# An MLP's first product by seven block products in place of eight, in a tuned fp32 transformer step

## Chip, cores and metric

One core of a Trainium2 chip runs the kernel. The metric is the device time of one launch in microseconds (us): the median of several runs. A measurement of this kernel tells about 0.2% from no change.

## What is computed

The reference is one step of a two-layer model on 640 tokens (128 of context, 512 latent) of width 1024. Each layer modulates its input, projects it, runs three kinds of attention heads, projects the result, and ends in a squared-ReLU MLP with 4096 features. The change lies in the MLP; `w_mlp1` is 1024 x 4096, `w_mlp2` is 4096 x 1024:

```
def _residual_tail(x, mix_heads, g_a, sh_m, sc_m, g_m, w_out, ln1_g, ln1_b, w_mlp1, w_mlp2, ln2_g, ln2_b):
    mix = jnp.concatenate(mix_heads, axis=-1) @ w_out
    x = _layer_norm(DN_ALPHA * x + g_a * mix, ln1_g, ln1_b)
    h = x * (1.0 + sc_m) + sh_m
    f = jnp.square(jax.nn.relu(h @ w_mlp1)) @ w_mlp2
    return _layer_norm(DN_ALPHA * x + g_m * f, ln2_g, ln2_b)
```

## The kernel before

Everything is fp32, and every large product is made from split operands: a number is the sum of a rounded part (hi, fp32r) and the rest (lo), and each product of two 128-deep blocks is three matmuls, hi·hi, lo·hi and hi·lo. `piece` (L366 to L373) makes a split weight: a DMA of 256 KB on SyncE's queue (SP) into one of four raw buffers (`wrawt`), ScalarE's cast to hi (L371), VectorE's subtraction to lo (L372), into one of eight buffers (`wst`). The split itself is

```
        nc.scalar.copy(ws[:, 0, :], raw)
        nc.vector.tensor_tensor(out=ws[:, 1, :], in0=raw, in1=ws[:, 0, :].bitcast(F32), op=ALU.subtract)
```

The MLP's input, transposed to features by tokens, is `Xt`: eight depth blocks of 128, hi and lo, 640 tokens. `to_feat` fills it one token tile of 128 at a time: four transposes on TensorE, four activations on ScalarE with the modulation's scale and bias, a cast (L509) and a subtraction (L510).

`mlp` (L1243 to L1313) goes through the 32 feature blocks in four chunks of eight. In a chunk `gemm_feat` (matmuls on L459) forms the first product: for a block two halves of 320 tokens, 24 matmuls of 320 columns each into a PSUM bank `gfeat`, 48 for a block. ScalarE copies each half out (L1257), VectorE squares the ReLU over 640 columns (L1258), ScalarE casts to hi (L1261) and GpSimd subtracts to lo (L1262): the split `f1T`, the stationary operand of the second product. That is `gemm_tok` (matmuls on L387), twice for a chunk, once for each half of 512 output columns: five token tiles, eight feature blocks, three matmuls of 512 columns each, 240 for a chunk. VectorE adds each finished tile to the residual from PSUM (`ln_add`, L1169 to L1176). In the first chunk VectorE also finishes the layer norm before (`ln_half`, L1237 and L1238, 20 operations of 128x512).

TensorE's order is written out by a planner when the program is built; the other engines' order comes from a scheduler, and each engine runs its own queue in order. After the last matmul of the second layer only the last tile's layer norm and its store remain.

Of the kernel before, what the change touches and what calls it, by code (L numbers as in the profile page):

```python
# [18 lines left out]
L = 2  # L19
D = 1024  # L20
NT = 5
TOK = 640
# [78 lines left out]
class Net:  # L101
# [277 lines left out]

    def gemm_tok(self, A, src, n, evac, by_block=False):  # L380

        nc = self.nc
        ws = [self.piece(src[:, k, :], n) for k in range(8)]

        def mm(o, t, k):
            for hl, wl in ((0, 0), (1, 0), (0, 1)):
                nc.tensor.matmul(  # L387
                    o, lhsT=A[YORDER[k] if A is self.Y else k][:, hl, t * 128 : (t + 1) * 128], rhs=ws[k][:, wl, :],
                    start=(k == 0 and hl + wl == 0), stop=(k == 7 and wl == 1),
                )  # L390

        if by_block:
# [101 lines left out]

    def to_feat(self, xh, t, A, B):

        nc = self.nc
        s = 1 if t == 0 else 0
        sl = slice(t * 128, (t + 1) * 128)
        for q in range(2):  # L500
            pt = self.tp.tile([128, 4, 128], F32, tag="t", name="pth")
            v = self.sm.tile([128, 4, 128], F32, tag="val", name="val", bufs=2)
            for j in range(4):
                k = 4 * q + j
                nc.tensor.transpose(pt[:, j, :], xh[:, k * 128 : (k + 1) * 128], self.ident)
# [223 lines left out]
    def mlstm(self, l):  # L729
# [119 lines left out]
        def chain():  # L849
# [27 lines left out]
            ce = self.sm.tile([128, 512], F32, name="ctxCe", bufs=1)  # L877
            nc.scalar.copy(ce[0:65, :], cp[0:65, :])
# [285 lines left out]
    def ln_add(self, r, q, o, gr, alpha, st=None, v=None):  # L1164
# [3 lines left out]
        v = o if v is None else v  # L1168
        nc.vector.tensor_tensor(out=v, in0=o, in1=gr[:, qs], op=ALU.mult)  # L1169
        o = v  # L1170
# [16 lines left out]
    def tail1(self, l, xsrc):  # L1187
# [9 lines left out]
        for t in range(NT):  # L1197
            self.R.append(self.qk.tile([128, D], F32, tag="qk", name="res"))
            nc.sync.dma_start(self.R[t], xsrc(t))
            st.append(self.sm.tile([128, 2, 6], F32, tag="bst", name="bst", bufs=NT))  # L1200

        def ev(q):
            def f(t, o):
                r = self.R[t]
                v = None if q else self.sm.tile([128, 512], F32, tag="val", name="wov", bufs=2)
                self.ln_add(r, q, o, g[:, int(t == 0)], ALPHA, st[t] if q else None, v)
                if q == 0 and t == NT - 1:
# [20 lines left out]
    def ln_half(self, l, i, h, dst=None):  # L1228
# [12 lines left out]
        self.use("V", 6.8)  # L1241

    def mlp(self, l):  # L1243
        nc, I, O = self.nc, self.I, self.O
        NC = 4
        last = l == L - 1
        R = self.R
        st = {}
        for c in range(NC):
            ft = []  # L1250
            n0 = 4 if c == 0 else 2
            first = [I["w1"][l, c * 8 + j] for j in range(n0)]
            rest = (g for j in range(n0, 8) for g in self.gemm_feat(I["w1"][l, c * 8 + j]))
            for j, g in enumerate(itertools.chain(self.gemm_feat(*first), rest)):
                f = self.tmp.tile([128, 2, 320], F32, tag="tmp", name="f1")
                for h in range(2):
                    nc.scalar.copy(f[:, h], g[h])  # L1257
                nc.vector.scalar_tensor_tensor(out=f, in0=f, scalar=0.0, in1=f, op0=ALU.max, op1=ALU.mult)  # L1258
                ft.append(self.yp.tile([128, 2, TOK], F32R, tag="y", name="f1T"))
                y = ft[j].rearrange("p a (h t) -> p a h t", h=2)  # L1260
                nc.scalar.copy(y[:, 0], f)  # L1261
                nc.gpsimd.tensor_tensor(out=y[:, 1], in0=f, in1=y[:, 0].bitcast(F32), op=ALU.subtract)  # L1262
                self.use("A", 0.75, self.use("V", 0.85, self.use("A", 0.9, self.T + 0.3)))
                if c == 0 and j in (3, 5):
                    self.ln_half(l, 0, j // 2 - 1)
            if c == 0:
                self.drain()
                if not last:
                    for i in range(3):
                        self.add(self.ada(l + 1, i, 512, 9.5), "ada")  # L1270
                gl = self.rowbc(self.pp, "p", self.ada_r[l][0:1, 5 * D : 6 * D])
                gc = self.rowbc(self.pp, "p", self.ada_r[l][1:2, 5 * D : 6 * D])
                if last:
                    lg = self.rowbc(self.pp, "p", I["ln"][l, 2:3, :])
                    lb = self.rowbc(self.pp, "p", I["ln"][l, 3:4, :])
            if c == NC - 1:
# [35 lines left out]
            for q in range(2):  # L1312
                self.gemm_tok(ft, I["w2"][l, c, q], 512, ev(q))  # L1313

# [68 lines left out]
def _pack(inp):  # L1383
# [89 lines left out]
```

## Time and profile before

| | |
|---|---|
| median of three runs | 1755.53 us (1752.77 to 1756.3) |
| profiled execution, its own time | 1749.54 us |
| its span, first to last instruction | 1747.8 us |
| mean granted TensorE clock | 0.98 of full speed |
| busy: TensorE, VectorE, ScalarE, GpSimd | 95%, 55%, 38%, 11% |
| MLP of the first layer begins, of the second | 418 us, 1281 us |

In the profile PE is TensorE, PEld its weight loads (beside PE), DVE VectorE, ACT ScalarE, POOL GpSimd, SP SyncE, which issues the loads. L459 is line 459 of the kernel. An idle time is given with what ended it: "0.51 <-ACT f L1257" is 0.51 us of waiting for ScalarE's write of `f` on line 1257. Matmul durations overlap in the pipeline, so the pace is read from the starts of successive groups.

### The profile page before, as it was taken

Reading aid. Unit: us, or ns where it says so; the run is one execution under the profiler, and the core shown is the slowest. Engines: PE = TensorE matmul, PEld = TensorE weight load, DVE = VectorE, ACT = ScalarE, POOL = GpSimd, SP = SyncE. Lnnn points to the kernel's source line nnn. Section 1 sums busy time; section 2 is a strip of 40 time slices with the busy share of each in tenths; the row PEclk is TensorE's granted clock in tenths of the full one; section 3 lists DMA queues with packets and bytes.
Section 4 is the critical chain, followed back from the end, with each engine's and each line's share of the span. In section 5 each row is a group of like instructions: output and inputs, shape, how many; then the busy total and the mean of one; then the engine's idle time right before and its main releaser. Section 6 shows DMA issues by size and latency. Waiting matters only on the chain.

```text
span 1747.8 us, 27703 instructions
## 1 busy us (share of the span) xinstructions
PE 1655.0 (95%) x10708; PEld 1439.3 (82%) x10708; DVE 954.8 (55%) x2105; ACT 660.0 (38%) x1482; POOL 189.8 (11%) x152
## 2 busy tenths in 40 slices
PE   5999799999999999999999997999999999999996
PEld 4988587778978878879889886878789898898985
DVE  3467766669533334233385777675784433433438
ACT  2342466655412313213253424665463142231420
POOL 0051000000300201101100510000002011020110
PEclk9999899999999999999999998999999999999998
DMA  8544433332344445433224331221322231221312
GB/s 312 200 154 142 138 130 114 108 115 90 110 140 168 163 145 170 151 103 109 67 88 143 98 98 41 74 73 60 127 80 90 65 98 62 91 73 49 103 44 83
DMA packets 105279, 195.23 MB, mean 112 GB/s; under 512 B 16410, under 2 KB 43034, under 8 KB 100028
## 3 DMA queue, kind: packets, MB, share of 16 engines
q1 hardware_dynamic: 105148, 193.47, 34.2%
q8 instruction: 84, 1.38, 0.3%
q14 instruction: 47, 0.39, 0.1%
HBM read 185.16 MB, written 8.26 MB: 111 GB/s over the span
## 4 chain that ended last, share of the span: by engine, by line
PE 74%; DVE 11%; issue 5%; DMA 4%; ACT 4%; POOL 1%; SPq 0%; DVEq 0%; ACTq 0%; POOLq 0%
PE gtok L387 34%; PE gfeat L459 30%; PE adaps L244 2%; PE o L1029 2%; PE ptp L1013 2%; ACT P L984 2%; PE s L970 1%; DMA adab<-in_b_ada 1%; DVE nm L977 1%; DVE wst L372 1%; DVE P L991 1%; DMA wrawt<-in_w_f 1%; DMA adaw<-in_w_ada 1%; PE mli L790 1%; POOL f1T L1262 1%
## 5 line engine op out<-in xcount | busy, mean ns | idle before, releaser
L459 PE MATMUL gfeat<-Xt,wst 128*128 128x320 f32 x4416 | 682.0, 313 | 6.6 <-ACT Xt L509 3.1
L459 PEld LDWEIGHTS gfeat<-Xt,wst 128*128 128x128 f32 x4416 | 655.2, 190 | 27.4 <-issue 11.6
L387 PE MATMUL gtok<-wst,f1T 128*128 128x512 f32 x1920 | 452.6, 396 | 0.9 <-ACT wst L371 0.8
L387 PEld LDWEIGHTS gtok<-wst,f1T 128*128 128x128 f32 x1920 | 359.1, 188 | 96.0 <-issue 8.4
L371 ACT CAST wst<-wrawt 128x512 fp32r<-128x512 f32 (+2 forms) x392 | 233.1, 604 | 513.9 <-PE gtok L387 253.2
L372 DVE TENSOR_TENSOR wst<-wrawt,wst 128x512 fp32r<-128x512 f32 (+2 forms) x392 | 272.7, 707 | 281.2 <-ACT wst L371 279.9
L1262 POOL TENSOR_TENSOR f1T<-f,f1T 128x640 fp32r<-128x640 f32 x64 | 105.1, 1642 | 976.5 <-ACT f1T L1261 973.8
L1169 DVE TENSOR_TENSOR gtok<-gtok,row 128x512 f32<-128x512 f32 x90 | 62.8, 698 | 226.5 <-PE gtok L387 226.1
L387 PE MATMUL gtok<-wst,Xt 128*128 128x384 f32 (+1 forms) x720 | 125.9, 330 | 7.4 <-DVE wst L372 7.4
L387 PEld LDWEIGHTS gtok<-wst,Xt 128*128 128x128 f32 x720 | 116.3, 193 | 11.3 <-DVE wst L372 8.6
L387 PE MATMUL gtok<-wst,yT 128*128 128x512 f32 x480 | 117.8, 399 | 1.6 <-DVE wov L1169 1.6
L1257 ACT COPY f<-gfeat 128x320 f32<-128x320 f32 x128 | 54.3, 426 | 154.0 <-PE gfeat L459 145.8
L387 PEld LDWEIGHTS gtok<-wst,yT 128*128 128x128 f32 x480 | 88.3, 188 | 22.9 <-DVE wov L1169 2.4
L984 ACT ACTIVATE P<-P,nm 128x512 f32<-128x512 f32 (+2 forms) x120 | 80.6, 673 | 33.5 <-DVE nm L979 15.7
L1258 DVE SCALAR_TENSOR_TENSOR f<-f 128x640 f32<-128x640 f32 x64 | 52.7, 823 | 53.3 <-ACT f L1257 53.3
L977 DVE TENSOR_REDUCE nm<-P 128x2 f32<-128x1024 f32 (+2 forms) x60 | 66.5, 1109 | 15.6 <-ACT P L1066 8.6
L244 PE MATMUL adaps<-adaw,cs 128*32 128x512 f32 (+1 forms) x576 | 56.1, 497 | 19.2 <-DMA adaw<-in_w_ada 19.1
L1021 ACT COPY PT<-ptp 128x512 f32<-128x512 f32 (+1 forms) x120 | 61.1, 542 | 24.9 <-PE ptp L1013 24.5
L1013 PE MATMUL ptp<-ident,P 128*128 128x128 f32 x432 | 64.9, 287 | 5.7 <-DVE P L991 5.3
L508 ACT ACTIVATE val<-pth,affB,affA 128x128 f32<-128x128 f32 x120 | 45.5, 469 | 52.1 <-DVE rsq L487 27.7
L1013 PEld LDWEIGHTS ptp<-ident,P 128*128 128x128 f32 x432 | 49.5, 145 | 18.0 <-issue 10.0
L1261 ACT CAST f1T<-f 128x640 fp32r<-128x640 f32 x64 | 46.6, 728 | 34.6 <-DVE f L1258 34.6
(210 smaller groups left out, 1270.7 us busy)
## 6 DMA issues: line engine op xcount, KB each, us to landing
wrawt<-in_w SPq DMA_DIRECT2D x256, 256.0 KB
adaw<-in_w_ada SPq DMA_DIRECT2D x40, 1024.0 KB
wrawt<-in_w_f SPq DMA_DIRECT2D x56, 256.0 KB
adaw<-in_w_ada SPq DMA_DIRECT2D x16, 512.0 KB
wrawt<-in_w_o SPq DMA_DIRECT2D x32, 256.0 KB
Dt<-md SPq DMA_DIRECT2D x40, 128.0 KB
nbias<-in_nbias SPq DMA_DIRECT2D x18, 256.0 KB
row<-adar SPq DMA_DIRECT2D x8, 512.0 KB
```

The lines of the kernel that those rows point to most:

```text
L244: self.nc.tensor.matmul(ps[32 * j : 32 * j + 32, :], lhsT=self.cs[:, k, :], rhs=w[:, j, :], start=(k == 0), stop=(k == 7))
L371: nc.scalar.copy(ws[:, 0, :], raw)
L372: nc.vector.tensor_tensor(out=ws[:, 1, :], in0=raw, in1=ws[:, 0, :].bitcast(F32), op=ALU.subtract)
L387: nc.tensor.matmul(o, lhsT=A[YORDER[k] if A is self.Y else k][:, hl, t * 128 : (t + 1) * 128], rhs=ws[k][:, wl, :], start=(k == 0 and hl + ...
L459: nc.tensor.matmul(g[i, h], lhsT=w[i][k // 4][:, wl, (k % 4) * 128 : (k % 4 + 1) * 128], rhs=self.Xt[:, k, hl, h * 320 : (h + 1) * 320], s ...
L977: nc.vector.tensor_reduce(out=nm[:, 0:2], in_=P[:, :, 0:nk], axis=AX.X, op=ALU.max, negate=True)
L984: nc.scalar.activation(P[:, h, 0:nk], P[:, h, 0:nk], AF.Exp, bias=nm[:, h : h + 1], accum_out=nm[:, 2 + h : 3 + h])
L1013: nc.tensor.transpose(pt[:, j, :], P[:, h, i * 128 : (i + 1) * 128], self.ident)
L1021: nc.scalar.copy(dst, src)
L1169: nc.vector.tensor_tensor(out=v, in0=o, in1=gr[:, qs], op=ALU.mult)
L1257: nc.scalar.copy(f[:, h], g[h])
L1262: nc.gpsimd.tensor_tensor(out=y[:, 1], in0=f, in1=y[:, 0].bitcast(F32), op=ALU.subtract)
```

## The change

The chunks become five: blocks 0 to 5, 6 to 11, 12 to 17, 18 to 23 and 24 to 31. The first six blocks of a layer are formed as before. The other 26 go in 13 pairs. The two blocks of a pair and the two halves of the depth make the weight a 2 x 2 matrix of blocks A, the two halves of the depth and of the tokens make the input a 2 x 2 matrix of blocks B; Strassen's method (in Winograd's form) gets the four blocks of the result from seven products instead of eight. A product is 12 matmuls of 320 columns. Its operands are A11, A12, A22 and four sums (S1 to S4) of weight blocks, and on the other side four blocks of the input and four sums (T1 to T4), three of which replace blocks.

`t_sums` and `t_split` make and split the T in the first chunk of a layer, once. `pair_weights` loads the four weight blocks of a pair, makes the sums and splits seven operands. `pairs` issues the products: some of them add up in PSUM; ScalarE copies a partial sum out, and VectorE adds another from PSUM. `relu2` now works on halves of 320 tokens in the pairs. The first pair of a chunk is prepared during the last second product of the chunk before (`inter`), and the last two products of a chunk's last pair stand inside the next second product (`between`). `to_feat` writes the fp32 input to `xf` tiles that the sums read; the token tile that straddles the two halves is cut in two. Gate rows, layer-norm rows and some scratch tiles move to other buffers, and w2 is stored by blocks.

```
     def gemm_tok(self, A, src, n, evac, by_block=False, between=None, ahead=2, inter=None):
...
+        if between is not None:
+            for t in range(ahead):
+                early[t] = self.gp.tile([128, 512], F32, tag="g", name="gtok")[:, 0:n]
+                for k in range(K - 2):
+                    mm(early[t], t, k)
...
+                    if (t, k) == (0, 1):
+                        between()
...
     def to_feat(self, xh, t, A, B, xf=None):
...
+                    a, b = max(t * 128, h * 320), min(t * 128 + 128, h * 320 + 320)
+                    if a < b:
+                        parts.append((xf[q, h][:, :, a - h * 320 : b - h * 320], a - t * 128, b - t * 128))
...
+                for v, a, b in parts:
+                    nc.scalar.activation(v[:, j, :], pt[:, j, a:b], AF.Identity, scale=A[:, s, k : k + 1], bias=B[:, s, k : k + 1])
...
+    def t_sums(self):
...
+        t3, t4 = [self.tmp.tile([128, 4, 320], F32, tag="tmp", name="tsum") for _ in range(2)]
+        nc.vector.tensor_tensor(out=b11, in0=b11, in1=b12, op=ALU.subtract)
+        nc.vector.tensor_tensor(out=t3, in0=b22, in1=b12, op=ALU.subtract)
+        nc.vector.scalar_tensor_tensor(out=b22, in0=b11, scalar=-1.0, in1=b22, op0=ALU.mult, op1=ALU.subtract)
+        nc.vector.scalar_tensor_tensor(out=t4, in0=b22, scalar=-1.0, in1=b21, op0=ALU.mult, op1=ALU.subtract)
...
+    def t_split(self, *which):
...
+            nc.scalar.copy(hi, self.t32[w])
+            nc.vector.tensor_tensor(out=lo, in0=self.t32[w], in1=hi.bitcast(F32), op=ALU.subtract)
...
+    def pair_weights(self, s1, s2):
...
+        def split(name, src):
+            w[name] = self.wsp.tile([128, 2, 512], F32R, tag="ws", name="wst")
+            nc.scalar.copy(w[name][:, 0, :], src)
+            nc.vector.tensor_tensor(out=w[name][:, 1, :], in0=src, in1=w[name][:, 0, :].bitcast(F32), op=ALU.subtract)
...
+        split("A11", a11)
...
+        split("A12", a12)
...
+        plus(s1, a21, a22)
+        plus(a21, a11, a21)
+        plus(a11, s1, a11)
+        plus(a12, a11, a12)
+        split("S2", a11)
...
+        split("S1", s1)
...
+        split("S3", a21)
...
+        split("A22", a22)
...
+        split("S4", a12)
...
+    def relu2(self, y, f, cols=slice(0, TOK)):
...
+        nc.vector.scalar_tensor_tensor(out=f, in0=f, scalar=0.0, in1=f, op0=ALU.max, op1=ALU.mult)
+        nc.scalar.copy(y[:, 0], f)
+        nc.gpsimd.tensor_tensor(out=y[:, 1], in0=f, in1=y[:, 0].bitcast(F32), op=ALU.subtract)
...
+    def pairs(self, srcs, ft):
...
+            self.product(a, w["A11"], X(0, 0), True, False)
+            nc.scalar.copy(f1[:, h0], a)
...
+            self.product(b, w["A12"], X(1, 0), True, True)
+            nc.vector.tensor_tensor(out=f1[:, h0], in0=b, in1=f1[:, h0], op=ALU.add)
...
+            self.product(a, w["S2"], T(2), False, False)
+            nc.scalar.copy(f1[:, h1], a)
...
+            self.product(c, w["S1"], T(1), True, False)
...
+            self.product(a, w["S3"], T(3), False, False)
+            nc.scalar.copy(f2[:, h1], a)
+            nc.vector.scalar_tensor_tensor(out=f2[:, h1], in0=f2[:, h1], scalar=-1.0, in1=c, op0=ALU.mult, op1=ALU.subtract)
...
+                self.product(a, w["A22"], T(4), False, True)
+                nc.scalar.activation(f2[:, h0], a, AF.Copy, scale=-1.0)
...
+                self.product(c, w["S4"], X(1, 1), False, True)
+                nc.vector.tensor_tensor(out=f1[:, h1], in0=c, in1=f1[:, h1], op=ALU.add)
...
+        chunks = [range(a, b) for a, b in itertools.pairwise((0, 6, 12, 18, 24, 32))]
...
+                    if j == 1:
+                        self.t_sums()
+                        self.t_split(1, 2)
...
+                self.t_split(3, 4)
...
+                self.gemm_tok(ft, [I["w2"][l, q, j] for j in blocks], 512, ev(q), between=left if q == 0 else None, ahead=2 if c < 4 else 3, inter=gen if q else None)
```

TensorE in the second layer's MLP, from the border of two chunks on (`gfeat`, `gpair`: first product; `gtok`: second). Before:

```order
L459 MATMUL gfeat<-Xt,wst 128x320 x288
L387 MATMUL gtok<-wst,f1T 128x512 x240
L459 MATMUL gfeat<-Xt,wst 128x320 x384
L387 MATMUL gtok<-wst,f1T 128x512 x240
L459 MATMUL gfeat<-Xt,wst 128x320 x384
```

Now, one chunk of three pairs; `tq` and the `f1T` read by `gpair` hold T operands:

```order
L393 MATMUL gtok<-wst,f1T 128x512 x162
L1348 MATMUL gpair<-Xt,wst 128x320 x12
L393 MATMUL gtok<-wst,f1T 128x512 x6
L1348 MATMUL gpair<-Xt,wst 128x320 x12
L393 MATMUL gtok<-wst,f1T 128x512 x6
L1348 MATMUL gpair<-f1T,wst 128x320 x12
L1348 MATMUL gpair<-tq,wst 128x320 x12
L1348 MATMUL gpair<-Xt,wst 128x320 x36
L1348 MATMUL gpair<-tq,wst 128x320 x12
L1348 MATMUL gpair<-f1T,wst 128x320 x12
L1348 MATMUL gpair<-Xt,wst 128x320 x12
```

Runs of one product are cut into products of 12, and the first two of a chunk have moved into the second product before it.

VectorE in the first chunk of the first layer, ahead of the fifth block's weights (`wst_4874` before, `wst_4896` now). Before:

```order
L510 TENSOR_TENSOR Xt_98<-val_4682,Xt_98 128x4x128
L1238 TENSOR_TENSOR res_3703<-res_3703,lnrow_4860 128x512
L1237 TENSOR_TENSOR res_3706<-res_3706,lnrow_4858 128x512
L1238 TENSOR_TENSOR res_3706<-res_3706,lnrow_4860 128x512
L372 TENSOR_TENSOR wst_4874<-wrawt_4872,wst_4874 128x512
L1258 SCALAR_TENSOR_TENSOR f1_4755<-f1_4755 128x640
```

Now:

```order
L1286 SCALAR_TENSOR_TENSOR xf_3710<-xf_3711,xf_3710 128x1280
L1269 TENSOR_TENSOR res_3700<-res_3700,lnrow_4882 128x512
L1287 SCALAR_TENSOR_TENSOR tsum_4807<-xf_3710,xf_3712 128x1280
L1356 SCALAR_TENSOR_TENSOR f1_4769<-f1_4769 128x640
L1301 TENSOR_TENSOR tq_4813<-xf_3711,tq_4812 128x1280
L1268 TENSOR_TENSOR res_3703<-res_3703,lnrow_4880 128x512
L1268 TENSOR_TENSOR res_3706<-res_3706,lnrow_4880 128x512
L1269 TENSOR_TENSOR res_3703<-res_3703,lnrow_4882 128x512
L1269 TENSOR_TENSOR res_3706<-res_3706,lnrow_4882 128x512
L1356 SCALAR_TENSOR_TENSOR f1_4800<-f1_4800 128x640
L372 TENSOR_TENSOR wst_4896<-wrawt_4894,wst_4896 128x512
```

The last two of the four sums (L1286, L1287; the other two stand above these rows), a split of 1280 columns and two ReLUs have come to stand ahead of the weights.

ScalarE in the second pair of a chunk of the second layer (`f1_13590` belongs to the first pair, `f1_13730` to the second). Before, in a chunk:

```order
L1257 COPY f1_15663<-gfeat_15613 128x320
L371 CAST wst_15873<-wrawt_15871 128x512
L1257 COPY f1_15663<-gfeat_15638 128x320
L371 CAST wst_15878<-wrawt_15876 128x512
L1261 CAST f1T_15667<-f1_15663 128x640
```

Now:

```order
L1427 ACTIVATE f1_13590<-gpair_13589 128x320
L1316 CAST wst_13790<-wrawt_13749 128x512
L1357 CAST f1T_12814<-f1_13590 128x320
L1408 COPY f1_13730<-gpair_13727 128x320
L1316 CAST wst_13811<-wrawt_13747 128x512
L1316 CAST wst_13830<-wsum_13806 128x512
L1316 CAST wst_13845<-wrawt_13751 128x512
L1357 CAST f1T_12813<-f1_13590 128x320
L1418 COPY f1_13730<-gpair_13727 128x320
```

Between two evictions of one bank (L1408, L1418) there are now three weight casts and the cast of a result; before, one weight cast stood between two evictions.

## Rows read from the trace of the kernel before

**Rows 1.** The page's busy times: us, share of the span, instructions.

```profile
span 1747.8 us, 27703 instructions
PE 1655.0 (95%) x10708; PEld 1439.3 (82%) x10708; DVE 954.8 (55%) x2105; ACT 660.0 (38%) x1482; POOL 189.8 (11%) x152
```

**Rows 2.** Timeline of PE, second layer's MLP: start, us, what, idle before.

```profile
1297.84 0.41 PE L459 MATMUL gfeat<-Xt,wst 128*128 128x320 f32 x1 [1.13 <-ACT Xt L509]
...
1302.72 11.03 PE L459 MATMUL gfeat<-Xt,wst 128*128 128x320 f32 x72 [0.51 <-ACT f L1257]
...
1342.26 55.83 PE L387 MATMUL gtok<-wst,f1T 128*128 128x512 f32 x240
1397.92 56.49 PE L459 MATMUL gfeat<-Xt,wst 128*128 128x320 f32 x384
1454.25 55.83 PE L387 MATMUL gtok<-wst,f1T 128*128 128x512 f32 x240
```

**Rows 3.** Chain of waits, from 1398 us: start, us, what.

```profile
1398.09 56.32 PE gfeat L459 x384
```

**Rows 4.** Windows: length, then busy PE, PEld, DVE, ACT, POOL; clock, DMA, GB/s.

```profile
1280.00:1342.00 62.00, 59.80 (x403) 58.42 (x402) 42.03 (x71) 30.98 (x64) 13.30 (x7) 1.00 0.35 106
1342.00:1398.00 56.00, 56.00 (x244) 45.45 (x244) 21.88 (x34) 9.76 (x16) 1.58 (x1) 1.00 0.19 59
1398.00:1454.00 56.00, 56.00 (x384) 56.00 (x383) 19.99 (x28) 21.84 (x40) 10.98 (x7) 1.00 0.30 92
```

**Rows 5.** Lines by form, 1280 to 1748 us: busy, mean ns, idle before.

```profile
L372 DVE TENSOR_TENSOR wst<-wrawt,wst 128x512 fp32r<-128x512 f32 x126 | 91.5, 731 | 112.9 <-ACT wst L371 112.8
...
L1258 DVE SCALAR_TENSOR_TENSOR f<-f 128x640 f32<-128x640 f32 x32 | 26.3, 823 | 25.5 <-ACT f L1257 25.5
L1172 DVE TENSOR_TENSOR res<-res,gtok 128x512 f32<-128x512 f32 x30 | 20.6, 686 | 0.7
L1223 DVE TENSOR_TENSOR res<-res,row 128x1024 f32<-128x1024 f32 x4 | 4.9, 1222 | 0.0
...
L371 ACT CAST wst<-wrawt 128x512 fp32r<-128x512 f32 x126 | 78.2, 623 | 200.5 <-PE gtok L387 86.3 <-DVE gtok L1169 60.9 <-PE gfeat L459 31.2
L1257 ACT COPY f<-gfeat 128x320 f32<-128x320 f32 x64 | 27.1, 425 | 74.5 <-PE gfeat L459 71.3 <-POOL f1T L1262 3.1
L1261 ACT CAST f1T<-f 128x640 fp32r<-128x640 f32 x32 | 23.3, 728 | 16.0 <-DVE f L1258 16.0
L508 ACT ACTIVATE val<-pth,affB,affA 128x128 f32<-128x128 f32 x16 | 6.0, 461 | 5.6 <-PE pth L505 5.6
```

**Rows 6.** Single lines: ns of one (least, median, most); L578 with its mean.

```profile
L372 DVE TENSOR_TENSOR wst<-wrawt,wst x19: 681/691/1640, 1397.9 to 1453.3; 128x512 fp32r<-128x512 f32 x19
L908 DVE SCALAR_TENSOR_TENSOR qkt<-gfeat,bcol,qkt x12: 541/545/551, 183.3 to 1176.2; 128x320 fp32r<-128x320 f32 x12
L1262 POOL TENSOR_TENSOR f1T<-f,f1T x32: 1557/1571/3612, 1304.4 to 1680.6; 128x640 fp32r<-128x640 f32 x32
L578 POOL TENSOR_TENSOR gmo<-gmo,ng 128x256 f32<-128x256 f32 x10 | 8.2, 815 | 110.1 <-ACT gmo L577 110.0
```

**Rows 7.** Timelines of DVE and POOL at two places: start, us, what.

```profile
1309.56 1.88 DVE L1238 TENSOR_TENSOR res<-res,lnrow 128x512 f32<-128x512 f32 x3
1311.37 0.68 DVE L1237 TENSOR_TENSOR res<-res,lnrow 128x512 f32<-128x512 f32 x1
...
1309.87 3.61 POOL L1262 TENSOR_TENSOR f1T<-f,f1T 128x640 fp32r<-128x640 f32 x1 [3.93 <-ACT f1T L1261]
...
1410.88 1.57 POOL L1262 TENSOR_TENSOR f1T<-f,f1T 128x640 fp32r<-128x640 f32 x1 [64.64 <-ACT f1T L1261]
...
1411.35 1.64 DVE L372 TENSOR_TENSOR wst<-wrawt,wst 128x512 fp32r<-128x512 f32 x1 [0.71 <-ACT wst L371]
```

**Rows 8.** Timeline of ACT: the first eviction of a chunk.

```profile
1401.70 0.43 ACT L1257 COPY f<-gfeat 128x320 f32<-128x320 f32 x1 [1.03 <-PE gfeat L459]
```

**Rows 9.** Waits of ACT, 418 to 646 us: us in total, times, longest.

```profile
ACT wst L371 <- DMA wrawt<-in_w: 12.0, 10, 3.0
```

More of the change, by code (lines that the diff above doesn't have):

```diff
@@ L378, in six, with gemm_tok @@
         return 6 * (n / 2300 + 0.008)
-    def gemm_tok(self, A, src, n, evac, by_block=False):
+    def gemm_tok(self, A, src, n, evac, by_block=False, between=None, ahead=2, inter=None):
         nc = self.nc
-        ws = [self.piece(src[:, k, :], n) for k in range(8)]
+        if not isinstance(src, list):
+            src = [src[:, k, :] for k in range(8)]
+        K = len(src)
+        ws = [self.piece(b, n) for b in src]
+        if inter is not None:
+            next(inter)
         def mm(o, t, k):
@@ L1168, in ln_add @@
         v = o if v is None else v
[L1169 removed]
+        nc.vector.tensor_tensor(out=v, in0=o, in1=gr, op=ALU.mult)
         o = v
@@ new lines, in t_split @@
+    def t_split(self, *which):
+        nc = self.nc
+        for w in which:
+            if w == 2:
+                self.t[2] = [v.rearrange("p a (k t) -> p (a k) t", k=2) for v in self.fb[6:]]
+            elif w != 3:
+                self.t[w] = [self.pp.tile([128, 4, 320], F32R, tag="p", name="tq") for _ in range(2)]
+            hi, lo = self.t[w]
+            nc.scalar.copy(hi, self.t32[w])
+            nc.vector.tensor_tensor(out=lo, in0=self.t32[w], in1=hi.bitcast(F32), op=ALU.subtract)
+            self.use("V", 2.0, self.use("A", 1.7))
@@ new lines, in product @@
+    def product(self, o, w, rhs, start, stop):
+        nc = self.nc
+        for k in range(4):
+            for hl, wl in ((0, 0), (1, 0), (0, 1)):
+                nc.tensor.matmul(o, lhsT=w[:, wl, k * 128 : (k + 1) * 128], rhs=rhs(k, hl), start=(start and k + hl + wl == 0), stop=(k == 3 and wl == 1), skip_group_check=not (start and stop))
+            if k % 2 == 1:
+                self.q(self.six(320))
+    def relu2(self, y, f, cols=slice(0, TOK)):
+        nc = self.nc
+        y, f = y[:, :, cols], f[:, cols]
+        nc.vector.scalar_tensor_tensor(out=f, in0=f, scalar=0.0, in1=f, op0=ALU.max, op1=ALU.mult)
+        nc.scalar.copy(y[:, 0], f)
+        nc.gpsimd.tensor_tensor(out=y[:, 1], in0=f, in1=y[:, 0].bitcast(F32), op=ALU.subtract)
@@ L1243, in mlp @@
     def mlp(self, l):
         nc, I, O = self.nc, self.I, self.O
-        NC = 4
+        chunks = [range(a, b) for a, b in itertools.pairwise((0, 6, 12, 18, 24, 32))]
+        self.fb = [self.yp.tile([128, 2, TOK], F32R, tag="y", name="f1T") for _ in range(8)]
+        NC = len(chunks)
         last = l == L - 1
@@ L1248, in mlp @@
         st = {}
[L1249 to L1265, printed above, removed]
-            if c == 0:
+        for c, blocks in enumerate(chunks):
+            ft, left = [], None
+            if c == 0:
+                first = [I["w1"][l, j] for j in range(4)]
+                rest = (g for j in range(4, 6) for g in self.gemm_feat(I["w1"][l, j]))
+                for j, g in enumerate(itertools.chain(self.gemm_feat(*first), rest)):
+                    f = self.sm.tile([128, 2, 320], F32, tag="val", name="f1", bufs=2)
+                    for h in range(2):
+                        nc.scalar.copy(f[:, h], g[h])
+                    ft.append(self.fb[j])
+                    self.relu2(ft[j], f.rearrange("p h t -> p (h t)"))
+                    self.use("A", 0.75, self.use("V", 0.85, self.use("A", 0.9, self.T + 0.3)))
+                    if j == 1:
+                        self.t_sums()
+                        self.t_split(1, 2)
+                    if j in (3, 5):
+                        self.ln_half(l, 0, j // 2 - 1)
+                self.t_split(3, 4)
                 self.drain()
@@ L1312, in mlp @@
             for q in range(2):
-                self.gemm_tok(ft, I["w2"][l, c, q], 512, ev(q))
+                gen = None
+                if q == 1 and c + 1 < NC:
+                    pre = []
+                    gen = self.pairs([I["w1"][l, j] for j in chunks[c + 1]], pre)
+                self.gemm_tok(ft, [I["w2"][l, q, j] for j in blocks], 512, ev(q), between=left if q == 0 else None, ahead=2 if c < 4 else 3, inter=gen if q else None)
     def layer(self, l):
```

142 lines of the change are left out of this document (124 added, 18 removed).

## The prediction

> **What bounds the kernel now.** I first read the busy shares: TensorE is busy for 1655.0 of 1747.8 us, VectorE for 55%, ScalarE for 38%, GpSimd for 11% [rows 1]. Such shares are means over stages, so next comes the timeline of TensorE in the MLP of the second layer [rows 2]. Its first chunk has short holes, for ScalarE's writes (1.13 us for the last inputs, 0.51 for an eviction); from 1342.26 us on there is no idle time: 240 matmuls of 512 columns, 384 of 320, in turn. The chain of waits says the same: its longest pieces are these runs on TensorE, as the one of 56.32 us [rows 3]. From the distance of the starts, 384 matmuls take 1454.25 − 1397.92 = 56.33 us, 146.7 ns each; 240 of 512 columns take 1397.92 − 1342.26 = 55.66 us, 231.9 ns each. [...] So TensorE alone sets the time here, and a matmul left out is worth its whole 146.7 ns, as long as no other engine takes over.
>
> **What it removes.** Two feature blocks took 96 matmuls, 96 × 0.1467 = 14.08 us; a pair now takes seven products of 12, 84 × 0.1467 = 12.32 us. There are 13 pairs in a layer: 2 × 13 × 12 = 312 matmuls less, **−45.8 us**, the most the change can give. The second product keeps its 960 matmuls a layer; one more border between chunks costs nothing, since TensorE goes over a border today without a hole [rows 2], and ten more evictions a layer (two operations of 128x512 each, 0.69 us like L1172, [rows 5]) lie in the second product's time, in which VectorE is busy for 21.88 of 56 us [rows 4].
>
> **What it adds to a pair.** VectorE: 7 splits and 4 weight sums, all 128x512 from two SBUF operands, at 0.69 us (median of L372, and L1172's mean, [rows 5, 6]): 11 × 0.69 = 7.59. Three additions that read PSUM, at L908's 0.545 [rows 6]: 1.64. Four squared ReLUs on 320 columns: no row has them; half of L1258's 0.823 is 0.41, the whole of a 512-column one 0.69 [rows 5]; nearer is the half, with some fixed part, 0.45 each: 1.8. Together 11.0 us of 12.32. ScalarE: 7 casts × 0.623, 4 copies × 0.425 and 4 casts of 320 columns, between half of 0.728 and 0.623, taken as 0.45: 7.9 us [rows 5]. GpSimd: 4 × 0.8 (half of L1262's median 1.571; L578 on 256 columns has a mean of 0.815, [rows 6]): 3.2 us. Each fits by itself. But VectorE's slack falls from 14.08 − 4 × 0.69 − 2 × 0.823 = 9.7 us to 1.3 us a pair, and its work does not run freely beside GpSimd's: at 1411.35 a split took 1.64 us, where 0.69 is usual, while GpSimd's subtraction ran from 1410.88 to 1412.45; and one of GpSimd's took 3.61 us while VectorE ran back to back from 1309.56 to 1312.05 [rows 7]. If whatever reads two SBUF operands can't run beside GpSimd's subtraction, that is 7.59 + 1.8 + 3.2 = 12.6 us a pair, 0.3 over TensorE's 12.32; if nothing on VectorE can, 11.0 + 3.2 = 14.2, 1.9 over. [...]
>
> The order matters too. ScalarE's eviction stands between weight casts in its queue, and the bank it reads takes the next product. A copy ends 0.7 us after the product's last matmul (24 matmuls from 1397.92 end at 1401.44; the copy runs from 1401.70 for 0.43, [rows 2, 8]), and one or two other products (1.76 or 3.52 us) cover that. With casts of 0.62 and their buffers, which VectorE frees, ahead of it, the play is used up in the second and third pair of a chunk. So a pair loses between 0 and 1.9 us; I take **0.5**, just above the 0.3 of the exclusion that the rows show: 26 × 0.5 = **+13 us** (0 to 49).
>
> **What it adds to the first chunk of a layer.** Four sums and four splits of 128x1280 on VectorE: from L1172's 0.686 at 512 and L1223's 1.222 at 1024 columns [rows 5], 1.49 each, 11.9 us in all. The window of today's first chunk has 42.03 us of VectorE in 62 [rows 4]. Two blocks fewer take 14.1 us of TensorE and 2 × (2 × 0.69 + 0.82) = 4.4 of VectorE away, so 42.0 − 4.4 + 11.9 = 49.5 us stand against 47.9, and GpSimd's 6 × 1.57 = 9.4 us want their share. In the first layer's queue the weights of the fifth block stand behind four sums, one split and two ReLUs, where none of these sums and splits stood before. What has no hurry (the last splits, the later layer norm) can slip into the second product. The half-tile cut in `to_feat` doubles the activations of one token tile: eight more, at most 0.461 each [rows 5], 3.7 us of ScalarE, next to the hole of 1.13 us [rows 2]. Bounds: 0 to 15.6 us a layer; I take three 1280-wide operations that stand in the way, 4.5, so **+9 us** for both.
>
> The rest costs nothing: four gate rows in place of two move the same bytes in chunk 0's shadow, GpSimd's halves are counted above, and after the last matmul the work is the same.
>
> **The sum:** −45.8 + 13 + 9 = −23.8 us. The profiled execution took 1749.54 us (span 1747.8), 6.0 below the median of the runs, 1755.53, and it would become 1725.7. Against the median the forecast is **1731.7 us**, with 1719 to 1744 for its own case.
>
> **The rivals.**
> *The cover holds.* VectorE's 11.0 us and the exclusion stay under TensorE, and the first chunk's additions slip into the second product, as 34 us of free VectorE there allow. Then −45.8 to −35 us: about 1713. For it: no engine by itself passes 12.32 us. Against: the 1.3 us of slack, and an order fixed when the program is built.
> *VectorE takes over (slower).* Place: the pairs. GpSimd's subtraction and VectorE exclude each other entirely, each stretched split holds up an eviction and so TensorE, and a pair costs 14.2 us. It decides from (45.8 − 9) ÷ 26 = 1.4 us a pair; at the full 1.9 the sum is −45.8 + 49 + 9 = +12, 1768 us. For it: the 3.61 us [rows 7] went on while VectorE had no gap. Against: VectorE waits for casts in most pairs (112.8 us of idle time before L372 ended by one, [rows 5]), and GpSimd fits there.
> *Raw weights come late.* The four raw buffers are now held until a pair's sums have been split, so the next loads start late, and ScalarE, in order, waits. Today it waits 10 times in the first layer's MLP, 12.0 us, the longest 3.0 [rows 9], beside 1 MB loads that the second layer lacks. One wait of 1.6 to 3 us in each of 13 pairs gives 21 to 39 us: 1753 to 1771, nothing gained.
>
> **How the numbers follow.** Chances: forecast 0.60, cover holds 0.17, VectorE takes over 0.13, raw weights 0.10 (of it 0.06 no change, 0.03 slower, 0.01 faster). Hence faster by over 0.2% (3.5 us, about what a measurement of this kernel can tell) 0.78, within it 0.06, slower 0.16. The range, 1712 to 1763, takes in the forecast's case, most of the full gain, the raw weights' lower half and the start of the slower case; beyond it lie some 0.06 below and 0.12 above.
>
> **What would show it.** Right: 156 fewer 320-column matmuls a layer; in a chunk's pairs VectorE above 85% busy, TensorE with holes of some tenths of a us ended by ScalarE's copies of `gpair` or by splits, about 0.5 us a pair; in the first chunk of each layer 3 to 6 us more of holes, ended by ScalarE's copies or by `wst`. Wrong: no holes in the pairs (cover holds), over 1.4 us a pair with VectorE full (slower), or holes ended by `wrawt` loads in the first layer alone. If GpSimd's half subtractions keep to 0.8 us and splits to 0.69, the exclusion plays no part and my pair term falls.

## The result, and the profile after

The changed kernel takes **1726.16 us** (median of four runs, 1724.02 to 1727.44) against 1755.61 us for the kernel before beside it: a ratio of 0.9834, 95% interval 0.9817 to 0.9851. The forecast was 1731.7 us in 1712 to 1763. Profile against profile the gain is 1749.54 − 1726.68 = 22.9 us; by the medians it is 29.5 us here and 26.2 in the repeat below (1752.01 − 1725.8). The forecast's sum was 23.8. The total is right, but two of its terms are not, and they nearly cancel.

The page's busy times of the changed kernel answer to [rows 1]:

```profile
PE 1620.9 (94%) x10396; PEld 1403.1 (81%) x10396; DVE 1177.1 (68%) x2477; ACT 716.8 (42%) x1640; POOL 214.7 (12%) x204
```

There are 312 matmuls fewer, and VectorE has 222 us more to do. Where the time went is read from TensorE's timeline in the second layer's MLP, which answers to [rows 2] (start, us, what, idle before):

```profile
1272.64 1.88 PE L477 MATMUL gfeat<-Xt,wst 128*128 128x320 f32 x11 [0.33 <-DVE Xt L539]
...
1287.96 0.41 PE L477 MATMUL gfeat<-Xt,wst 128*128 128x320 f32 x1 [1.14 <-ACT Xt L538]
1290.17 5.17 PE L477 MATMUL gfeat<-Xt,wst 128*128 128x320 f32 x23 [1.80 <-DVE Xt L539]
1295.86 3.78 PE L477 MATMUL gfeat<-Xt,wst 128*128 128x320 f32 x24 [0.52 <-ACT f L1454]
1300.70 21.38 PE L477 MATMUL gfeat<-Xt,wst 128*128 128x320 f32 x144 [1.06 <-ACT f L1454]
1321.92 3.65 PE L393 MATMUL gtok<-wst,f1T 128*128 128x512 f32 x15
1327.34 0.50 PE L393 MATMUL gtok<-wst,f1T 128*128 128x512 f32 x1 [1.77 <-ACT f1T L1357]
1329.18 38.09 PE L393 MATMUL gtok<-wst,f1T 128*128 128x512 f32 x152 [1.34 <-POOL f1T L1358]
1367.12 1.92 PE L1348 MATMUL gpair<-Xt,wst 128*128 128x320 f32 x12
...
1383.98 1.94 PE L1348 MATMUL gpair<-f1T,wst 128*128 128x320 f32 x12
...
1396.32 1.94 PE L1348 MATMUL gpair<-f1T,wst 128*128 128x320 f32 x12
...
1656.70 54.41 PE L393 MATMUL gtok<-wst,f1T 128*128 128x512 f32 x234
```

From 1329.18 us to the end there is not one hole; pairs follow each other every 1396.32 − 1383.98 = 12.34 us, which is their 84 matmuls at 146.7 ns. All the loss stands before 1367 us. From the first matmul of an MLP to its last, the first layer's takes 472.0 us (485.5 before) and the second's 440.45 (452.95 before): 13.5 and 12.5 us less, where 156 × 0.1467 = 22.9 were taken out of each. So the first chunks cost 9.4 and 10.4 us, 19.8 in all. The MLPs together are 26.0 us shorter, which is near what the medians of the repeat say. What lies outside the MLPs takes 3 us more in this profile than in that of before, but 0.8 us more in the second profiles of both kernels (811.0 against 810.2); so the 3 us are, at least for the most part, the scatter of single executions.

The idle time accounts for half of that. In the second layer it adds up to 0.33 + 1.14 + 1.80 + 0.52 + 1.06 + 1.77 + 1.34 = 7.96 us up to 1329.18, against 2.2 before; in the first layer to 0.52 + 2.85 + 1.30 + 1.35 = 6.02 against 0.8. First layer of the changed kernel:

```profile
441.70 3.78 PE L477 MATMUL gfeat<-Xt,wst 128*128 128x320 f32 x24 [0.52 <-ACT f L1454]
448.32 24.07 PE L477 MATMUL gfeat<-Xt,wst 128*128 128x320 f32 x144 [2.85 <-ACT f L1454]
472.22 3.64 PE L393 MATMUL gtok<-wst,f1T 128*128 128x512 f32 x15
477.16 0.49 PE L393 MATMUL gtok<-wst,f1T 128*128 128x512 f32 x1 [1.30 <-ACT f1T L1357]
479.00 9.04 PE L393 MATMUL gtok<-wst,f1T 128*128 128x512 f32 x26 [1.35 <-POOL f1T L1358]
487.97 1.06 PE L244 MATMUL adaps<-adaw,cs 128*32 128x512 f32 x8
```

In its first layer the kernel before has holes of 0.52 and 0.24 us; in the second, beside those of [rows 2], one of 0.24 and this one, with the usual time of 23 matmuls:

```profile
1298.57 3.64 PE L459 MATMUL gfeat<-Xt,wst 128*128 128x320 f32 x23 [0.31 <-DVE Xt L510]
```

The other half shows in the length of the groups behind the holes: 26 matmuls of 512 columns take 487.97 − 479.00 = 8.97 us where 26 × 0.2319 is 6.03. The windows of that stretch give the reason (columns as in [rows 4]: the granted clock stands behind POOL):

```profile
482.00:485.00 3.00, 3.00 (x8) 2.32 (x8) 0.00 (x0) 0.00 (x0) 0.00 (x0) 0.50 0.01 3
485.00:488.00 3.00, 3.00 (x17) 2.14 (x17) 1.28 (x2) 0.00 (x0) 0.00 (x0) 1.00 0.00 0
```

TensorE was idle for 2.65 of 3.1 us and then ran at half clock, granted 0.50, with nothing left to wait for: 2.9 us more. The same 0.50 stands behind the hole of 2.85 us (window 448.4 to 454.2; 144 matmuls in 23.90 us where 21.12 are usual, 2.8 more) and in the second layer behind those of 1.14 and 1.80 (1290.6 to 1293.9; 23 in 5.17 against 3.64, 1.5) and of 1.77 and 1.34 us (1328.9 to 1334.8; 152 in 37.94 against 35.25, 2.7). In the kernel before, the clock is 1.00 in both MLPs (420 to 860 and 1283 to 1734 us). Together 9.9 us of slow clock beside 11.0 us more of holes: 20.9, near the 19.8 by the lengths.

What made the longest hole is told by three timelines of the changed kernel, of VectorE, GpSimd and ScalarE:

```profile
441.79 0.82 DVE L1356 SCALAR_TENSOR_TENSOR f<-f 128x640 f32<-128x640 f32 x1
442.53 1.48 DVE L1301 TENSOR_TENSOR tq<-xf,tq 128x1280 fp32r<-128x1280 f32 x1
443.93 1.28 DVE L1268 TENSOR_TENSOR res<-res,lnrow 128x512 f32<-128x512 f32 x2
445.14 1.28 DVE L1269 TENSOR_TENSOR res<-res,lnrow 128x512 f32<-128x512 f32 x2
```

```profile
443.45 4.36 POOL L1358 TENSOR_TENSOR f1T<-f,f1T 128x640 fp32r<-128x640 f32 x1 [150.73 <-ACT f1T L1357]
```

```profile
447.84 0.43 ACT L1454 COPY f<-gfeat 128x320 f32<-128x320 f32 x1 [4.47 <-POOL f1T L1358]
```

A split of 1280 columns and four layer-norm operations run on VectorE without a gap; GpSimd's subtraction, issued among them, ends 1.4 us after the last of them and takes 4.36 us instead of 1.57; the next eviction wants the buffer that it reads. It is the picture of [rows 7], with a buffer and TensorE behind it.

Two more lines, of VectorE in the second layer, belong to the hole of 1.80 us there: the subtraction of the last token tile (L539), which that hole waits for, starts when the sum ahead of it ends. Three lines of ScalarE belong to the holes at 1327.34 and 1329.18:

```profile
1288.03 1.48 DVE L1284 TENSOR_TENSOR xf<-xf 128x1280 f32<-128x1280 f32 x1
1289.43 0.69 DVE L539 TENSOR_TENSOR Xt<-xf,Xt 128x512 fp32r<-128x512 f32 x1
```

```profile
1319.36 0.62 ACT L371 CAST wst<-wrawt 128x512 fp32r<-128x512 f32 x1 [3.10 <-DMA wrawt<-in_w]
1323.00 1.27 ACT L1300 CAST Xt<-tsum 128x1280 fp32r<-128x1280 f32 x1
1324.68 0.43 ACT L1454 COPY f<-gfeat 128x320 f32<-128x320 f32 x1
```

TensorE was done with the last block at 1321.92, and ScalarE copied its second half at 1324.68 (before, 0.2 us after the product, at 1342.46). In between stood a cast of T, and ahead of that casts that had waited 5.8 us in three times for raw weights, 3.10 in the longest. SyncE's queue, which loads them, was in its turn waiting mostly for VectorE to release buffers.

In the pairs there is no such thing. The single lines of the changed kernel (least, median, most in ns) and the window of two pairs and a bit:

```profile
L1317 DVE TENSOR_TENSOR wst<-wrawt,wst x156: 674/684/1376, 502.2 to 1645.1; 128x512 fp32r<-128x512 f32 x156
L1419 DVE SCALAR_TENSOR_TENSOR f<-f,gpair x26: 473/481/489, 535.3 to 1653.6; 128x320 f32<-128x320 f32 x26
L1358 POOL TENSOR_TENSOR f1T<-f,f1T x116: 871/886/4359, 443.5 to 1659.1; 128x320 fp32r<-128x320 f32 x104, 128x640 fp32r<-128x640 f32 x12
```

```profile
1373.40:1401.60 28.20, 28.20 (x193) 28.19 (x192) 24.60 (x41) 16.40 (x34) 8.62 (x8) 1.00 0.35 107
```

VectorE is busy for 24.60 of 28.20 us, 87%, as foretold, and TensorE never waits.

### The profile page after: what moved, and what is told of

Its sections match the earlier page's. It is cut to its first block, busy times and chain, and to the rows that moved or that the text cites. A ratio compares the mean times of both kernels' runs of the same rounds, so it can differ in the third digit from the quotient of the medians.

```text
span 1724.8 us, 27638 instructions
## 1 busy us (share of the span) xinstructions
PE 1620.9 (94%) x10396; PEld 1403.1 (81%) x10396; DVE 1177.1 (68%) x2477; ACT 716.8 (42%) x1640; POOL 214.7 (12%) x204
## 3 DMA queue, kind: packets, MB, share of 16 engines
q8 instruction: 82, 1.34, 0.3%
## 4 chain that ended last, share of the span: by engine, by line
PE 75%; DVE 11%; ACT 5%; DMA 4%; issue 3%; POOL 1%; SPq 1%; DVEq 0%; ACTq 0%; POOLq 0%
PE gtok L393 35%; PE gpair L1348 19%; PE gfeat L477 10%; PE adaps L244 2%; PE o L1058 2%; PE ptp L1042 2%; ACT P L1013 2%; PE s L999 1%; DVE nm L1006 1%; DVE wst L372 1%; DVE P L1020 1%; PE mli L819 1%; DMA adab<-in_b_ada 1%; DMA nbias<-in_nbias 1%; ACT PT L1050 1%
## 5 line engine op out<-in xcount | busy, mean ns | idle before, releaser
L477 PE MATMUL gfeat<-Xt,wst 128*128 128x320 f32 x1920 | 316.0, 320 | 11.9 <-ACT f L1454 4.9
L477 PEld LDWEIGHTS gfeat<-Xt,wst 128*128 128x128 f32 x1920 | 292.8, 194 | 23.9 <-ACT f L1454 6.0
L1358 POOL TENSOR_TENSOR f1T<-f,f1T 128x320 fp32r<-128x320 f32 (+1 forms) x116 | 130.3, 1125 | 932.3 <-ACT f1T L1357 822.2
L372 DVE TENSOR_TENSOR wst<-wrawt,wst 128x512 fp32r<-128x512 f32 (+2 forms) x288 | 197.9, 701 | 69.4 <-ACT wst L371 67.6
L1348 PE MATMUL gpair<-Xt,wst 128*128 128x320 f32 x1248 | 195.1, 309 | 0.0
L1348 PEld LDWEIGHTS gpair<-Xt,wst 128*128 128x128 f32 x1248 | 186.2, 188 | 6.2 <-issue 2.5
L1316 ACT CAST wst<-wrawt 128x512 fp32r<-128x512 f32 x156 | 94.5, 620 | 196.3 <-DVE gtok L1198 106.5
L1317 DVE TENSOR_TENSOR wst<-wrawt,wst 128x512 fp32r<-128x512 f32 x156 | 112.5, 733 | 34.2 <-ACT wst L1316 34.0
L1348 PE MATMUL gpair<-tq,wst 128*128 128x320 f32 x624 | 100.9, 310 | 0.0
L1348 PEld LDWEIGHTS gpair<-tq,wst 128*128 128x128 f32 x624 | 93.8, 188 | 4.8 <-issue 4.2
L1356 DVE SCALAR_TENSOR_TENSOR f<-f 128x320 f32<-128x320 f32 (+1 forms) x116 | 68.6, 593 | 26.2 <-ACT f L1427 19.3
```

Of the source, the lines that this page charges most:

```text
L477: nc.tensor.matmul(g[i, h], lhsT=w[i][k // 4][:, wl, (k % 4) * 128 : (k % 4 + 1) * 128], rhs=self.Xt[:, k, hl, h * 320 : (h + 1) * 320], s ...
L1316: nc.scalar.copy(w[name][:, 0, :], src)
L1317: nc.vector.tensor_tensor(out=w[name][:, 1, :], in0=src, in1=w[name][:, 0, :].bitcast(F32), op=ALU.subtract)
L1348: nc.tensor.matmul(o, lhsT=w[:, wl, k * 128 : (k + 1) * 128], rhs=rhs(k, hl), start=(start and k + hl + wl == 0), stop=(k == 3 and wl == 1 ...
```

## The experiments

Unless a run's text says otherwise, it is the changed kernel with an edit; ratios are to the kernel before on the same chip.

**The T sums moved behind the first product.** In `mlp` the sums leave the place after the second block; the first one waits for the eviction of token tile 0 of the second product, by a factor of one made from it, and one split follows each later tile:

```
-                    if j == 1:
-                        self.t_sums()
-                        self.t_split(1, 2)
...
-                self.t_split(3, 4)
...
+                    if c == 0 and q == 0 and t == 0:
+                        one = self.sm.tile([128, 1], F32, name="one1", bufs=1)
+                        nc.vector.tensor_scalar(one, r[:, 0:1], 0.0, 1.0, ALU.mult, ALU.add)
+                        self.t_sums(one)
+                    elif c == 0 and q == 0:
+                        self.t_split(t)
```

The author's theory: the first chunk's loss comes from these 1280-column operations on VectorE's and ScalarE's queues, so the holes of 2.85 us at 448 us and 1.80 us at 1290 us go with the half clock behind them, and the two pairs of holes at the start of the second product get shorter: 8 to 18 us in all, 1708 to 1718 us.

> The four T sums and their splits leave the first chunk's first product: the first sum waits for the eviction of the first token tile of the second product (a multiplication by one made from that tile), and one split follows each later tile. [...] Rival (the holes come from the layer norm's operations and from the short chunk, the sums only fill gaps): within 3 us of 1726.

Measured: 1711.6 us, ratio 0.977 (0.9754 to 0.9787). Once more on another chip, where a ratio of 0.976 to 0.979, both MLPs within 0.5 us of this trace's and no half clock in them were expected:

> [...]

Measured: 1708.53 us, ratio 0.9747 (0.973 to 0.9765), a little better than the 0.976 to 0.979 expected; the MLPs 462.4 and 431.2 us in the first trace, 462.5 and 431.9 in the second (the last 0.2 over what was expected). TensorE in the second layer, first of these runs:

```profile
1283.22 0.41 PE L477 MATMUL gfeat<-Xt,wst 128*128 128x320 f32 x1 [1.14 <-ACT Xt L538]
1283.99 3.64 PE L477 MATMUL gfeat<-Xt,wst 128*128 128x320 f32 x23 [0.36 <-DVE Xt L539]
1288.15 25.11 PE L477 MATMUL gfeat<-Xt,wst 128*128 128x320 f32 x168 [0.52 <-ACT f L1454]
```

The holes left there are nearly those of the kernel before, and 23 matmuls take their 3.6 us again; in both layers the 168 matmuls behind the hole of 0.52 us have the second product begin 24.9 us after their start, where 168 × 0.1467 is 24.6: there is no stretch at half clock. Against the changed kernel both MLPs together are 18.9 us shorter. So the sums' place, not their cost, made the loss; the holes and the slow clock went together here.

**A third buffer** for the squared ReLU of every third block of the first chunk:

```
-                    f = self.sm.tile([128, 2, 320], F32, tag="val", name="f1", bufs=2)
+                    f = self.sm.tile([128, 2, 320], F32, tag="sv" if j % 3 == 2 else "val", name="f1", bufs=1 if j % 3 == 2 else 2)
```

The author's theory: the eviction at 447.84 us waited for a buffer that GpSimd's subtraction of 4.36 us still read, so that wait, the hole of 2.85 us and the 6.83 us at half clock behind it go: 1719 to 1721 us. The rival: VectorE's queue itself is late, and the eviction would wait for the squared ReLU: 1725 to 1727 us.

> Every third feature block of the first chunk gets a third buffer for its squared ReLU (a scratch tile that is free there). [...]

Measured: 1721.29 us, 0.3 above the theory's range, ratio 0.9826 (0.9809 to 0.9842), which can't be told from the change's 0.9834. In the trace the MLPs are 1.9 and 2.8 us shorter than the changed kernel's. The 2.85 us hole is gone as expected (first chunk's first product 44.7 us, was 50.8), but of these 6.1 us most come back at once: the second product's weights are now late. The longest of four such holes:

```profile
469.00 1.89 PE L393 MATMUL gtok<-wst,f1T 128*128 128x512 f32 x7 [2.20 <-DVE wst L372]
```

The buffer was the last link of the wait; behind it stood VectorE's load, as the run before shows.

**Two token tiles first** in the first chunk's second product:

```
-                self.gemm_tok(ft, [I["w2"][l, q, j] for j in blocks], 512, ev(q), between=left if q == 0 else None, ahead=2 if c < 4 else 3, inter=gen if q else None)
+                self.gemm_tok(ft, [I["w2"][l, q, j] for j in blocks], 512, ev(q), between=(left or (lambda: None)) if q == 0 else None, ahead=2 if c < 4 else 3, inter=gen if q else None)
```

The author's theory: the last block's split is late by 2.65 us in the first layer and 3.1 us in the second, and 6.83 us at half clock follow; both go, 12 us at most: 1714 to 1718 us. The rival: the clock falls in this stretch whatever stands before it, and only the holes go: 1720 to 1721 us.

> In the first chunk the second product starts with four of the six blocks for two token tiles, as the later chunks do, so that the last blocks are wanted 2.8 us later. [...]

Measured: 1718.43 us, ratio 0.9812 (0.9795 to 0.9828); 0.4 us above the theory's range. From the first matmul of the second product to the first pair it takes 44.1 and 39.5 us, 49.5 and 45.2 in the changed kernel: 5.4 and 5.7 less, of which the holes make half. The time at half clock in the first MLP falls from 13.7 us to 6.8, in the second from 10.2 to 3.4; what is left stands behind the earlier holes, which are still there. So the clock follows the holes here, not the stage.

**Four more sums a pair**, to find where VectorE becomes the bound:

```
-        plus(s1, a21, a22)
+        for _ in range(5):
+            plus(s1, a21, a22)
```

> The first weight sum of each pair is formed five times instead of once: four more operations of 128x512 on VectorE in each pair, 4 x 0.61 = 2.4 us by the pitch of such operations back to back. Theory (VectorE has 12.32 - 10.75 = 1.6 us of slack in a pair by its busy share of 87%): it becomes the bound by 0.8 us a pair, 26 x 0.8 = 21 us, so about 1747 us. Rival of the forecast (work of VectorE and GpSimd does not run side by side, so the slack is already gone): 26 x 2.4 = 62 us, 1788 us. Other rival (pairs are not near VectorE's limit): 1726 us.

Measured: 1749.44 us, ratio 0.9996 (0.998 to 1.0012): the whole gain is gone. In the second layer, from the first pair to the last run of `gtok`:

```profile
1373.65 1.92 PE L1349 MATMUL gpair<-Xt,wst 128*128 128x320 f32 x12
1674.70 54.41 PE L393 MATMUL gtok<-wst,f1T 128*128 128x512 f32 x234
```

That is 301.05 us against 1656.70 − 1367.12 = 289.58: 11.5 us over 13 pairs, 0.88 each, where 0.8 was expected; 3.4 us of the stretch are at half clock. TensorE's longest waits are for VectorE's splits, 5.4 us in 5 times; casts and an eviction make 2.1 more, and none is for a result of GpSimd:

```profile
PE gpair L1349 <- DVE wst L1317: 5.4, 5, 1.3
```

**The same four sums without GpSimd's part.** The pairs leave out the subtraction, so their result has no low part:

```
-        nc.gpsimd.tensor_tensor(out=y[:, 1], in0=f, in1=y[:, 0].bitcast(F32), op=ALU.subtract)
+        if lo:
+            nc.gpsimd.tensor_tensor(out=y[:, 1], in0=f, in1=y[:, 0].bitcast(F32), op=ALU.subtract)
```

> Four more sums a pair as in the run with them, but GpSimd's subtraction is left out in the pairs, so the low part of their result is not made. VectorE's demand by pitch is 15 x 0.61 + 3 x 0.40 + 4 x 0.42 = 12.0 us a pair, under TensorE's 12.32; with GpSimd beside it a pair took 0.76 us more than 12.32. Theory (the exclusion of GpSimd's subtraction and VectorE's two-operand work makes the difference): the 0.76 us go, the MLPs get 15 to 20 us shorter than with it, about 1726 us. Rival (queue order and waits for casts make it, GpSimd has no part): within 4 us of that run.

Measured: 1734.48 us, ratio 0.9886 (0.9865 to 0.9907). The MLPs are 16.9 us shorter than with GpSimd's part, in the theory's range; the about 1726 us were not reached. The stretch is now 1664.90 − 1372.87 = 292.03 us:

```profile
1372.87 1.92 PE L1349 MATMUL gpair<-Xt,wst 128*128 128x320 f32 x12
1664.90 54.41 PE L393 MATMUL gtok<-wst,f1T 128*128 128x512 f32 x234
```

9.0 of the 11.5 us have gone with GpSimd's work; 2.5 stay, 0.19 a pair, and what makes them no run separates (in the first layer 4.3 of 12.0 stay). VectorE's sums (`wsum`, L1320, by form from 1360 to 1680 us) show directly what GpSimd costs them, first with its subtraction, then without:

```profile
L1320 DVE TENSOR_TENSOR wsum<-wrawt 128x512 f32<-128x512 f32 x65 | 48.0, 739 | 4.4 <-DMA wrawt<-in_w 2.9
```

```profile
L1320 DVE TENSOR_TENSOR wsum<-wrawt 128x512 f32<-128x512 f32 x64 | 44.1, 689 | 5.0 <-DMA wrawt<-in_w 3.7
```

GpSimd's subtraction does cost VectorE time in the pairs: a sum takes 739 ns in the mean beside it and 689 without, at most 1370 and 694; the changed kernel has room for that. The edit also frees the buffers that GpSimd reads, but with GpSimd's part in place no wait of TensorE in the pairs names one of them.

**The change again, and the three edits together** (sums moved, two tiles first, third buffer), without and with two more sums a pair:

Expected of the change were a ratio of 0.981 to 0.986 and half clock in both first chunks, and no holes where that is missing.

> [...]

> The three edits together: T sums and splits in the second product, two token tiles begun first, a third buffer. Theory (after the sums have left, the first chunk loses only the hole of some 2 us at the start of the second product, 39.73 us from its first matmul to the pairs in the second layer where 162 matmuls of 231.9 ns need 37.6): 1 to 4 us less than with the sums moved alone, a ratio to the kernel before of 0.975 to 0.9765. Rival (with two tiles first the sums come too late for the first pair, or hold evictions up): a ratio of 0.978 or more.

> On top of those three edits the first weight sum of each pair is formed three times: two more operations on VectorE in each pair, 1.2 us by their pitch. Theory (1.6 us of slack a pair): hidden, within 3 us of the run without them. Rival (queueing costs before VectorE is full): 0.3 to 0.8 us a pair, 8 to 21 us more.

Measured: 1725.8 us, ratio 0.9848 (0.9833 to 0.9863), with the same 13.7 and 10.2 us at half clock; then 1709.8 us, 0.975 (0.9734 to 0.9766); then 1714.37 us, 0.9782 (0.9767 to 0.9797). The three edits gain no more than the sums alone (0.977 and 0.9747): with two tiles first the eight operations of 1280 columns come close together and the weights of the product's second half stand behind them, a hole of 2.63 us with a slow clock behind it (0.76 on average from 1329 to 1336 us):

```profile
1332.05 13.18 PE L393 MATMUL gtok<-wst,f1T 128*128 128x512 f32 x49 [2.63 <-DVE wst L372]
```

The two extra sums make the MLPs 2.7 and 2.8 us longer, 0.21 us a pair: neither hidden, as the theory had it, nor 0.3 or more. The slack is not free up to its edge.

**The sums in both halves**, beside the third buffer and two tiles first. Two sums and two splits follow the first tile of the second product's first half, the others that of its second half:

```
+                    if c == 0 and t == 0:
+                        one = self.sm.tile([128, 1], F32, name="one1", bufs=1)
+                        nc.vector.tensor_scalar(one, r[:, q * 512 : q * 512 + 1], 0.0, (1.0, -1.0)[q], ALU.mult, ALU.add)
+                        (self.t_sums, self.t_sums2)[q](one)
+                    elif c == 0 and t in (1, 2):
+                        self.t_split(((1, 3), (2, 4))[q][t - 1])
```

The author's theory: the hole of 2.63 us in the second layer, with 3.41 us at half clock behind it, and one of 1.52 us in the first go, 4 to 6 us less than with all sums in the first half: a ratio of 0.972 to 0.9735.

> Two token tiles first and the third buffer, with the T work cut in two: two sums and two splits after the first tile of the second product's first half, the others after the first tile of its second half. [...] Rival (the second half's VectorE is too full with the first pair's weights, so the hole moves to the first pair): 0.975 or more.

Measured: **1700.61 us**, ratio 0.9708 (0.9692 to 0.9724), better than expected and better than both kernels. From 1273.73 us TensorE has no hole:

```profile
1273.73 28.27 PE L477 MATMUL gfeat<-Xt,wst 128*128 128x320 f32 x191 [0.33 <-DVE Xt L539]
1301.84 39.18 PE L393 MATMUL gtok<-wst,f1T 128*128 128x512 f32 x168
```

The MLPs take 461.2 and 429.5 us, 47.8 less than before: the whole 45.8, and a little of the holes that the kernel before had.

**The kernel before again**, for what lies ahead of the first MLP:

> The kernel before once more, for its trace: the changed kernel's first MLP began 3.3 us later than that of before (412.7 against 409.4 us from the first matmul), though nothing ahead of it was changed that TensorE waits for by plan. Theory (spread between executions): the start of the first MLP moves by 1 us or more against the first trace of this kernel. Rival (the change delays something ahead of the MLP): it stays within 0.5 us of 409.4.

Measured: 1750.98 us in one run; the first MLP begins 410.0 us after the first matmul, 0.6 later than in the first trace, which decides for neither. The changed kernel and its variants began it between 410.5 and 416.1 us. Whether the change delays something there by a us or two, or the executions scatter, stays open.

## Why the prediction came out right, point by point

- **What is removed, −45.8 us: right.** Pairs run at 12.34 us each, and with the first chunk mended the MLPs are 47.8 us shorter.
- **The pair term, +13 us: wrong, it is 0.** The step that failed is "Together 11.0 us of 12.32": it added the durations of VectorE's operations, 0.69 us each. Back to back they follow each other faster: three take 1.88 us [rows 7], and in a pair of the changed kernel VectorE's timeline has

```profile
1467.34 0.48 DVE L1432 TENSOR_TENSOR f<-gpair,f 128x320 f32<-128x320 f32 x1
1467.74 0.68 DVE L1320 TENSOR_TENSOR wrawt<-wrawt 128x512 f32<-128x512 f32 x1
1468.34 0.68 DVE L1317 TENSOR_TENSOR wst<-wrawt,wst 128x512 fp32r<-128x512 f32 x1
1468.94 0.48 DVE L1356 SCALAR_TENSOR_TENSOR f<-f 128x320 f32<-128x320 f32 x1
1469.34 0.68 DVE L1317 TENSOR_TENSOR wst<-wsum,wst 128x512 fp32r<-128x512 f32 x1
```

  where an operation of 0.68 us takes 0.60 from start to start and one of 0.48 takes 0.40. By that a pair needs 11 × 0.60 + 7 × 0.40 = 9.4 us, and the work on two SBUF operands with GpSimd's 4 × 0.886 comes to 6.6 + 1.6 + 3.5 = 11.7, under 12.32 and not the 12.6 of the prediction. That GpSimd holds VectorE up is as predicted in kind (a split up to 1376 ns, and at most 696 in the run with no GpSimd in the pairs; 9.0 us between the runs with and without its part), only it fits. Even 11.7 is an upper estimate, since it gives every subtraction of GpSimd a time of its own: with four more sums the same count says 1.8 us a pair over 12.32, and 0.88 was measured; with two more it says 0.6, and 0.21 was measured. The operations that read PSUM are left out of it by what the trace shows: the 26 of L1419, which read PSUM and one SBUF operand, never took over 489 ns, though 8 of them ran beside a subtraction of GpSimd.
- **The first chunk, +9 us: right in its mechanism, half its size.** It cost 19.8 us. The holes, 11.0 us more than before, are near the forecast. What the sum did not hold is the clock after them, 9.9 us. The weights of the fifth block, which the prediction put in the way, were not what TensorE waited for; it was an eviction behind GpSimd, the inputs of the last token tile behind a sum, and the last block's result behind a cast of T and behind casts that waited for raw weights.
- **The rivals.** "The cover holds" was right in the pairs and wrong in the first chunk: the sums could have slipped into the second product, as the moved ones show, but the queue had them ahead. "VectorE takes over" has its point where it was put: 0.88 us a pair with four more sums is 23 us over 26 pairs, and with the first chunks' loss nothing of the gain is left. "Raw weights come late" has no part in the pairs, and no hole above is released by a load; but in the first chunk ScalarE waits for raw weights, and the evictions behind it come late.
- **The total** was within 1 us by the profiles (−22.9 against −23.8) because +13 that did not come stands against 10.8 that was missing in the first chunk and 3 outside the MLPs. That is luck: the MLPs alone gained 26.0 us, and of the last 3 us the second profiles of both kernels show 0.8.

## What to carry to other kernels

Count an engine that works without gaps by the distance of the starts, not by durations (0.60 against 0.68 us an operation here), and count two engines that were seen to hold each other up as one queue for an upper estimate (11.7 us here, in a pair of 12.32 that showed no wait). When a change takes TensorE's work away and gives VectorE some, look where VectorE was already without a gap; one-time preparation belongs in the stage with room, and here it had been queued as soon as its inputs were there, ahead of what was urgent. Price a hole in TensorE with what the clock did after it in the trace: here 9.9 us beside 11.0 us of holes.

## What was not expected of the hardware

Holes cost more than themselves in the changed kernel. Two that add up to 2.65 us in 3.1 us were followed by half clock (granted 0.50) that cost 2.9 us more; one of 2.85 us by 2.8, 1.77 and 1.34 us by 2.7, 1.14 and 1.80 us by 1.5. Holes of 1.14, 0.36 and 0.52 us within 6 us, in the kernel with the sums moved, left the pace as it was (23 matmuls in 3.64 us). A GpSimd subtraction, 1.57 us at the median before, took 4.36 us (443.45 to 447.81) beside a run of VectorE's operations of 0.6 to 1.5 us each that ended at 446.42: it ended only after the whole run, not after the one that it met.
